# Loads of w_out earlier, two operands' low parts by DMA, another pool for a product's bank

## The chip, the cores and the metric

The kernel runs on one core of one Trainium2 chip. The metric is the device time of one execution in microseconds (us): 1637.95 us, the median of three runs (1635.71 to 1638.52).

## The reference, cut to what matters

One layer of a hybrid encoder block over 1024 tokens of width 1024, with 16 meta tokens ahead of them, all in float32. After the two mixers (an mLSTM, whose output is y_a, and neighbourhood attention, y_b) come the steps that the change touches:

```python
mix = g_a * (y_a @ w_branch_a) + g_b * (y_b @ w_branch_b)
h = h + mix @ w_out
z = rms_norm(h, norm2_g) @ w_ff1
h = h + jnp.square(jax.nn.relu(z)) @ w_ff2
```

In the kernel w_branch_a is `w_a`, w_branch_b is `w_b`, w_ff1 is `w1` and w_ff2 is `w2`.

## The kernel before, in words

**Products of three.** Every large product is made of matmuls of fp32r operands that are split into a high and a low part: high by high, high by low, low by high (`mm3`). The high part is a cast on ScalarE. The low part is made in one of two ways (`low`, L1157): VectorE subtracts the high part from the value, or ScalarE writes the negated high part and a DMA on POOL's queue adds the value to it in place (`by_dma`). `hilo` (L1151) makes both parts. For w_out's operands `Rows.split` (L1331) does the same; its DMA is L1338.

**Seven products for eight.** From w_a on, each product of matrices is done by a scheme of seven products (1 to 7) of half-sized operands. `ASIDE` names the left operand of each: A11, A12, A22 are quarters, S1 to S4 sums of quarters that `s_parts` (L1201) makes. `Cols` (L1227) handles one column block of w_a (four, `cols_a`) or w1 (sixteen, `cols_1`): a product is 12 matmuls into one bank of PSUM. `Rows` (L1314) handles w_out (`out_p`) and w2, each product in two halves q, of 24 matmuls into four banks.

**The order.** A list `seq` holds all these products as (object, i, q): 28 of w_a, then from n_o = 28 on 14 of w_out (1, 2, 6, 5, 3, 7, 4, each for q = 0 and 1), then from n_1 = 42 on those of w1, of whose first five blocks the products 1 and 2 come first. The loop at the end walks the list; before product n it runs what is hooked to n (`hook`, L1612), then has the operands of a few products ahead prepared (`ensure`, L1388), and then writes out the matmuls (`mul`). The operands of w_out are prepared from n_o on (`ready`), and in the kernel before this is also where w_out's eight loads are written (`Rows.load`, called by `parts`; `out_quarters`, L1463, with the load itself in L1470). x's first four loads (`load_x2`, L1476) are hooked to n_o - 7 to n_o - 4.

**The planner.** This order gives priorities only. A planner simulates the engines and queues when the program is built: it issues what is ready, by priority, and fixes the order on each engine and queue. The chip then works each queue strictly in that order. So a load can begin long before the place where it is written, once its buffer is free.

**Buffers.** Nearly all operands, loads and results live in 44 buffers of one kind (`slot`, 128 x 1040 values). PSUM has eight banks: a pool of two (`gbank`) and one of six (`bank`, also for the transposes and for w_out's four). `Cols.mul` takes its bank from the pool of two for the products 1 and 2.

**Ahead of w_a.** The eight blocks of w_b are multiplied by y_b in a loop over j. Their results go from PSUM into `gbq` on VectorE (`ev_b`, L1186), and after each second j to DRAM (`gbd<-gbq`, L1191). In the same loop y_a is loaded (`yq`, L1402), its quarters A11 (j = 3) and A12 (j = 4) are split (tiles `ya30`, `ya31`, `ya40`, `ya41`, with h or l), and from j = 5 on `s_parts` makes the sums (`ys`).

In the trace most instructions have the line of a helper, L137, and are told apart by tiles: `pow01l` is w_out's operand for q = 0, product 1, low part; `poz01l` the left one; `wo` are the raw loads.

Of the kernel before, what the change touches and what calls it, by code (L numbers as in the profile page):

```python
# [182 lines left out]
def build(tc, A, taps=None):  # L183
# [18 lines left out]
    def slot(name, dt=F32):  # L202
        return sp.tile([128, L], dt, name=name, tag="S")

    def bank(name="x"):
        return psx.tile([128, 512], F32, name=name, tag="x")

    def gbank(name="g"):
        return psg.tile([128, 512], F32, name=name, tag="g")
# [31 lines left out]
    def mm3(out, ah, al, bh, bl, first, last):  # L241
        PE.matmul(out, ah, bh, start=first, stop=False)
        PE.matmul(out, ah, bl, start=False, stop=False)
        PE.matmul(out, al, bh, start=False, stop=last)
# [154 lines left out]
    def gemm_block(wh, wl, n0, n, ks=KC, act=(xh, xl), off=0):  # L399
        ps = gbank()[:, 0:n]  # L400
        m = slice(n0 - off, n0 - off + n)
        for k in range(ks):
            c = slice(k * 128, (k + 1) * 128)
            mm3(ps, wh[:, c], wl[:, c], act[0][k][:, m], act[1][k][:, m], k == 0, k == ks - 1)
            yield 3 * n * 0.000422
        return ps

    def first_block(wh, wl, n0, n):

        ps = gbank()[:, 0:n]  # L410
        m = slice(n0, n0 + n)
        for k in range(KC):
            c = slice(k * 128, (k + 1) * 128)
            PE.matmul(ps, wh[:, c], xh[k][:, m], start=k == 0, stop=False)
            PE.matmul(ps, wh[:, c], xl[k][:, m], start=False, stop=False)
        for k in range(KC):
            ins = PE.matmul(ps, wl[:, k * 128:(k + 1) * 128], xh[k][:, m], start=False, stop=k == KC - 1)
        return ps, ins

    def gemm_in(wi, blocks, evac, ks=KC, act=(xh, xl), off=0, ahead=1):  # L420
        wh, wl = W.get(wi, ahead)
        for b, (n0, n) in enumerate(blocks):
            ps = yield from gemm_block(wh, wl, n0, n, ks, act, off)
            evac(b, n0, n, ps)

    def run(gen):
        while True:
            try:
                next(gen)
            except StopIteration as e:  # L430
                return e.value
# [23 lines left out]
    for b, ts in enumerate(groups):  # L455
        n0, n = b * 256, min(256, L - b * 256) if b < 3 else L - 768
        ps = run(gemm_block(gh, gl, n0, n))
# [5 lines left out]
        for j in (0, 1):  # L463
            ps, ins = first_block(*wx[j], n0, n)
# [89 lines left out]
    ya = {}  # L554
# [579 lines left out]
    def late(name, dt=F32):  # L1134
        return LP.tile([128, 1024], dt, name=name, tag="r", bufs=7)
# [6 lines left out]
    def lo(e):  # L1142
        return slice(e * 512, e * 512 + 512)
# [7 lines left out]
    def hilo(src, name, by_dma=False):  # L1151
        h_, l_ = slot(name + "h", F32R), slot(name + "l", F32R)
        SC.copy(h_[:, 0:S], src[:, 0:S])
        low(l_[:, 0:S], src[:, 0:S], h_[:, 0:S], by_dma)
        return h_, l_

    def low(l_, src, h_, by_dma):  # L1157
        if by_dma:

            SC.activation(l_, h_.bitcast(F32), AF.Copy, scale=-1.0)  # L1160
            nc.gpsimd.dma_start(l_, src, accum_op=OP.add)
        else:
            rest(l_, src, h_, share_gp[0])
# [9 lines left out]
    def load_gb(p):  # L1173
        for h_ in range(2):
            gb[p, h_] = slot(f"gbq{p}{h_}")
            dma(gb[p, h_][:, 0:1024].rearrange("p (e t) -> p e t", e=2),
                gated[2 * p:2 * p + 2, :, h_ * 512:h_ * 512 + 512].rearrange("e p t -> p e t"))
# [8 lines left out]
    def ev_b(j):  # L1186
        def ev(b, n0, n, ps):
            o = gb[j // 2, b][:, lo(j % 2)]
            V.scalar_tensor_tensor(o, o, 1.0, ps, OP.add, OP.mult)
            if j % 2 == 1:  # L1190
                dma(gbd[j // 2, b], gb.pop((j // 2, b))[:, 0:1024])  # L1191
        return ev
# [34 lines left out]
    class Cols:  # L1227
# [56 lines left out]
            return self.t["sp"]  # L1284

        def mul(self, i, q):
            ps = gbank("pf") if i in (1,2) else bank("pf")
            c = self.c.pop(i)
            for k in range(4):
                h_, l_ = self.z[ASIDE[i], k // 2]  # L1290
                m = lo(k % 2)
                mm3(ps, c[:, k * 128:(k + 1) * 128], c[:, 512 + k * 128:512 + (k + 1) * 128], h_[:, m], l_[:, m],
                    k == 0, k == 3)
            t = self.t
            if i == 1:
                pu = late("pu")
                t["p1"], t["u2"] = pu[:, 0:512], pu[:, 512:1024]
                SC.copy(t["p1"], ps)
            elif i == 2:
                self.out(0, 0, ps, t["p1"])  # L1300
            elif i == 6:
                V.tensor_add(t["u2"], ps, t["p1"])
            elif i == 7:
                t["u3"] = self.spare()[:, 0:512]
                V.tensor_add(t["u3"], ps, t["u2"])
            elif i == 5:
                self.out(1, 1, ps, t["u3"])
                V.tensor_add(t["u2"], ps, t["u2"])
            elif i == 4:
                self.out(1, 0, ps, t["u3"])  # L1310
            else:
                self.out(0, 1, ps, t["u2"])
# [72 lines left out]
    seq, before, after, ready = [], {}, {}, {}  # L1385
# [10 lines left out]
    za = {}  # L1396
    yq = {}

    def load_ya(h_):
        for i in range(4):  # L1400
            yq[h_, i] = slot(f"yq{h_}{i}")
            dma(yq[h_, i][:, 0:1024].rearrange("p (e t) -> p e t", e=2),  # L1402
                yad[2 * i:2 * i + 2, :, h_ * 512:h_ * 512 + 512].rearrange("e p t -> p e t"))
# [14 lines left out]
    for j in range(8):  # L1418
        if j == 7:
            cols_a[0].prep(2, 0)  # L1420
        if j in (1, 3):
            load_gb(j // 2 + 2)
        run(gemm_in(w_b[j], NBS, ev_b(j), 4, ([t[0] for t in ybs], [t[1] for t in ybs])))
        if j in (1, 2):
            load_ya(j - 1)
        if j in (3, 4):
            for i in (0, 1):
                za["A11" if j == 3 else "A12", i] = hilo(yq[0, 2 * (j - 3) + i], f"ya{j}{i}")
        if j >= 5:
            next(sy)  # L1430
    ybs = None
# [42 lines left out]
    def load_x2(t):  # L1474
        x_ = slot(f"hx{t}")
        dma(x_[:, 0:D], A["x"][t * 128:(t + 1) * 128, :])  # L1476
        hx.append(x_)
# [38 lines left out]
    out_p = Rows("po", out_quarters, out_o, late, True)  # L1516
# [95 lines left out]
    def hook(d, n, fn):  # L1612
        d.setdefault(n, []).append(fn)

    group(cols_a, NE1)
    n_o = len(seq)
# [20 lines left out]
    for t in range(4):  # L1637
        hook(before, n_o - 7 + t, lambda t=t: load_x2(t))
        hook(before, n_o + 2 + t, lambda t=t: load_x2(t + 4))
    ready[n_1] = n_o + 11  # L1640

    def z_half(k0):
        zt(0, range(k0, k0 + 4))
        for i in range(2):
            zz["A11" if k0 == 0 else "A12", i] = hilo(zf[0, k0 // 2 + i], f"za{k0}{i}")
# [98 lines left out]
```

## Time and profile before

| | us |
|---|---|
| median of three runs | 1637.95 |
| lowest and highest | 1635.71, 1638.52 |
| the profiled execution | 1635.56 |
| its span, first to last instruction | 1633.8 |
| TensorE busy in the span | 1589.9 (97%) |
| VectorE, ScalarE, POOL busy | 1129.7, 897.5, 231.1 |
| TensorE's granted clock, mean | 0.994 |

Times in the views are counted from the span's start. A busy TensorE is not TensorE at its peak. A wait is the idle time of an engine right before an instruction, put down to what ended last before it.

### The profile page before, as it was taken

To read this page: it belongs to the slowest core of one execution; us is meant where nothing else is said; L and a number is where in the kernel's file an instruction comes from. 1 tells how busy PE (TensorE), PEld (TensorE's weight loads), DVE (VectorE), ACT (ScalarE), POOL (GpSimd) and SP (SyncE) were. 2 spreads that over 40 slices of the span, in tenths; PEclk is the share of its full clock that TensorE was granted. 3 is DMA by queue.
4 is the path that set the end of the run, shared out by engine and by line. 5 is a ranking of instruction groups with operands and counts; after the bars stand their busy time and mean duration, and the time that the engine had idled before them with its cause. 6 is when DMAs were issued, how large, how long until landed. Compare 5 with 4: busy or idle time off the path is not lost.

```text
span 1633.8 us, 22503 instructions
## 1 busy us (share of the span) xinstructions
PE 1589.9 (97%) x8081; PEld 1351.2 (83%) x8081; DVE 1129.7 (69%) x2191; ACT 897.5 (55%) x1572; POOL 231.1 (14%) x387
## 2 busy tenths in 40 slices
PE   7999999999999999999999999999999999999999
PEld 7878889888989998888778788788888878888887
DVE  4537766574758687774398968965655595969597
ACT  5566676576748586864242656644444467344350
POOL 5110212112143223121100121000000001010000
PEclk9999999999999999999999999999999999999999
DMA  4362664636374444354933972133323639282733
GB/s 156 88 136 66 153 146 127 147 78 169 64 183 95 102 89 109 70 119 140 291 136 130 270 187 83 53 133 123 123 111 116 229 107 311 57 247 67 219 83 98
DMA packets 78415, 221.07 MB, mean 135 GB/s; under 512 B 11336, under 2 KB 21960, under 8 KB 78304
## 3 DMA queue, kind: packets, MB, share of 16 engines
q1 hardware_dynamic: 54976, 138.76, 24.3%
q0 software_dynamic: 23328, 80.88, 24.0%
q8 instruction: 64, 1.05, 0.3%
q14 instruction: 47, 0.39, 0.1%
HBM read 168.12 MB, written 38.76 MB: 127 GB/s over the span
## 4 chain that ended last, share of the span: by engine, by line
PE 79%; issue 8%; DMA 5%; ACT 4%; DVE 4%; POOL 1%; POOLq 0%; DVEq 0%; ACTq 0%
PE pf L137 41%; PE g L137 27%; DMA wl<-w_in 3%; PE po L137 2%; PE pt L137 2%; PE pp L137 1%; PE ps L137 1%; PE pi L137 1%; PE pn L137 1%; PE pu L137 1%; DMA xcl<-xc 1%; DVE gt L137 1%; DMA pow01l<-w_out 1%; PE pk L137 1%; PE pq L137 1%
## 5 line engine op out<-in xcount | busy, mean ns | idle before, releaser
L137 PE MATMUL g<-xh,wh 128*128 128x512 f32 (+3 forms) x784 | 290.7, 371 | 7.3 <-DVE xm L137 3.9
L137 PE MATMUL g<-xh,wl 128*128 128x512 f32 (+3 forms) x784 | 287.6, 367 | 5.4 <-DMA wl<-w_in 5.4
L137 PE MATMUL g<-xl,wh 128*128 128x512 f32 (+3 forms) x784 | 287.3, 366 | 0.0
L137 PEld LDWEIGHTS g<-xh,wh 128*128 128x128 f32 x784 | 148.9, 190 | 25.7 <-DVE xm L137 4.2
L137 PEld LDWEIGHTS g<-xh,wl 128*128 128x128 f32 x784 | 148.9, 190 | 25.0 <-DMA wl<-w_in 7.0
L137 PEld LDWEIGHTS g<-xl,wh 128*128 128x128 f32 x784 | 149.1, 190 | 16.8
L137 ACT ACTIVATE zq<-zq 128x512 f32<-128x512 f32 x128 | 80.7, 633 | 123.7 <-DVE zq L137 121.9
L137 DVE TENSOR_TENSOR acc<-acc,pf 128x512 f32<-128x512 f32 x96 | 64.1, 681 | 40.5 <-PE pf L137 40.3
L137 DVE CUSTOM_DVE_ANT_0 P<-ps,bt 128x400 f32<-128x400 f32 x64 | 36.0, 570 | 41.1 <-issue 24.2
L137 ACT ACTIVATE wl<-wh 128x1024 fp32r<-128x1024 f32 (+1 forms) x50 | 49.3, 987 | 24.1 <-DMA wh<-w_b 8.6
L174 POOL DMA_DIRECT2D wl<-w_in x42 | 38.4, 914 | 137.5 <-ACT wl L137 73.6
L137 DVE SCALAR_TENSOR_TENSOR C<-C,decb,pu 128x258 f32<-128x258 f32 x52 | 23.6, 479 | 39.3 <-PE pu L137 39.0
L137 DVE TENSOR_TENSOR pu<-pf,pu 128x512 f32<-128x512 f32 x40 | 27.4, 686 | 30.1 <-PE pf L137 30.0
L137 ACT ACTIVATE P<-P,mn 128x400 f32<-128x400 f32 x64 | 40.2, 630 | 10.9 <-DVE mn L137 10.4
L1338 POOL DMA_DIRECT2D f0w02l<-w_ff x1 | 0.9, 911 | 313.8 <-DVE zq L137 313.8
L137 DVE TENSOR_TENSOR zq<-pf,sp 128x512 f32<-128x512 f32 x32 | 22.1, 691 | 32.4 <-PE pf L137 32.4
L137 DVE TENSOR_SCALAR P<-P,sm 128x384 f32<-128x384 f32 (+1 forms) x128 | 38.5, 364 | 0.9
L137 DVE TENSOR_TENSOR zq<-pf,pu 128x512 f32<-128x512 f32 x32 | 22.0, 687 | 22.6 <-PE pf L137 22.6
L137 DVE TENSOR_TENSOR ptl<-pp,pth 128x384 fp32r<-128x384 f32 x64 | 35.5, 555 | 2.8 <-ACT pth L137 2.1
L137 ACT CAST pth<-pp 128x512 fp32r<-128x512 f32 x60 | 34.0, 581 | 5.4 <-PE pp L137 5.2
L137 PE MATMUL pp<-con,P 128*128 128x128 f32 x256 | 34.9, 272 | 0.0
L137 ACT ACTIVATE nn<-pi,tm 128x258 f32<-128x258 f32 x60 | 27.0, 473 | 14.1 <-PE pi L137 14.1
(2400 smaller groups left out, 4765.2 us busy)
## 6 DMA issues: line engine op xcount, KB each, us to landing
wh<-w_in POOLq DMA_DIRECT2D x42, 512.0 KB, 5.5
wl<-w_in POOLq DMA_DIRECT2D x42, 512.0 KB, 5.8
z2d<-zq SPq DMA_DIRECT2D x32, 512.0 KB, 3.0
zr<-z2d SPq DMA_DIRECT2D x32, 512.0 KB, 4.6
w2r<-w_ff SPq DMA_DIRECT2D x32, 512.0 KB, 13.0
bt<-rpbd SPq DMA_DIRECT2D x256, 32.0 KB, 2.8
xcl<-xc POOLq DMA_DIRECT2D x8, 520.0 KB, 5.2
ra<-rowd SPq DMA_DIRECT2D x8, 512.0 KB, 4.3
```

The costliest lines, as they stand in the source:

```text
L137: return fn(out, *a, **k)
L174: self.nc.gpsimd.dma_start(l[:, 0:w], src, accum_op=OP.add)
L1338: nc.gpsimd.dma_start(l_[:, 0:S], src, accum_op=OP.add)
```

## The change

It does three things. w_out's loads for q = 0 and q = 1 are hooked to the products n_o - 9 and n_o - 4. The low parts of A11 and A12 of y_a are made by ScalarE and a DMA on POOL's queue and not by VectorE: four times one negation and one transfer of 512 KB. And in `Cols.mul` product 2 takes its bank from the pool of six, so that the pool of two is left to product 1.

```diff
         def mul(self, i, q):
-            ps = gbank("pf") if i in (1,2) else bank("pf")
+            ps = gbank("pf") if i == 1 else bank("pf")
...
         if j in (3, 4):
             for i in (0, 1):
-                za["A11" if j == 3 else "A12", i] = hilo(yq[0, 2 * (j - 3) + i], f"ya{j}{i}")
+                za["A11" if j == 3 else "A12", i] = hilo(yq[0, 2 * (j - 3) + i], f"ya{j}{i}", True)
...
         hook(before, n_o - 7 + t, lambda t=t: load_x2(t))
         hook(before, n_o + 2 + t, lambda t=t: load_x2(t + 4))
     ready[n_1] = n_o + 11
+    for q in range(2):
+        hook(before, n_o - 9 + 5 * q, lambda q=q: out_p.load(q))
```

## Rows read from the trace of the kernel before

**Rows 1.** The page, part 1: span, and busy time of TensorE.

```profile
span 1633.8 us, 22503 instructions
...
PE 1589.9 (97%) x8081; PEld 1351.2 (83%) x8081; DVE 1129.7 (69%) x2191; ACT 897.5 (55%) x1572; POOL 231.1 (14%) x387
```

**Rows 2.** Waits of TensorE from 760 us to the end: us in total, times, longest us.

```profile
PE pf L137 <- ACT pow02h L137: 3.3, 1, 3.3
PE g L137 <- DVE gbq L137: 2.9, 4, 1.3
...
PE pf L137 <- ACT pu L137: 1.4, 2, 0.8
```

**Rows 3.** Timeline of TensorE, w_out's first products: start, us, instruction [idle before <-releaser].

```profile
911.78 1.09 PE L137 MATMUL pf<-pow01h,poz01h 128*128 128x512 f32 x4
916.13 0.49 PE L137 MATMUL pf<-pow02h,poz02h 128*128 128x512 f32 x1 [3.26 <-ACT pow02h L137]
916.90 0.50 PE L137 MATMUL pf<-pow01l,poz01h 128*128 128x512 f32 x1 [0.28 <-DMA pow01l<-w_out]
...
923.45 0.39 PE L137 MATMUL pf<-pow11l,poz11h 128*128 128x512 f32 x1
```

**Rows 4.** Stretches: length, busy PE, PEld, DVE, ACT, POOL; granted clock, DMA share, GB/s.

```profile
800.00:810.00 10.00, 8.80 (x38) 6.55 (x37) 5.20 (x6) 2.62 (x3) 0.87 (x1) 1.00 1.07 371
810.00:820.00 10.00, 8.65 (x38) 6.59 (x36) 7.48 (x9) 1.68 (x2) 1.41 (x2) 1.00 0.42 104
890.00:900.00 10.00, 10.00 (x45) 8.10 (x44) 7.77 (x13) 3.92 (x6) 0.00 (x0) 1.00 0.64 221
900.00:910.00 10.00, 10.00 (x45) 8.13 (x44) 9.66 (x12) 3.05 (x3) 0.86 (x1) 1.00 1.03 413
918.00:920.00 2.00, 2.00 (x6) 1.63 (x5) 2.00 (x4) 0.06 (x1) 0.43 (x1) 0.50 1.07 223
920.00:922.00 2.00, 2.00 (x7) 1.56 (x7) 1.97 (x3) 1.97 (x3) 0.00 (x0) 0.68 1.08 213
```

**Rows 5.** Timeline of SP's DMA issues, 893 to 912 us.

```profile
893.68 2.43 SPq L1476 DMA_DIRECT2D hx<-x  x3
...
897.17 2.28 SPq L1470 DMA_DIRECT2D wo<-w_out  x4
...
901.10 4.17 SPq L1470 DMA_DIRECT2D wo<-w_out  x4
```

**Rows 6.** Timeline of ScalarE, 897 to 916 us.

```profile
904.95 1.05 ACT L137 CAST pow01h<-wo 128x1024 fp32r<-128x1024 f32 x1 [5.81 <-DMA wo<-w_out]
```

**Rows 7.** Tile pow01l: its low-part transfer and its time to landing.

```profile
L1338 POOL DMA_DIRECT2D pow01l<-w_out x1: 861/861/861, 907.5 to 907.5; - x1
...
DMA to landing us min/median/max: 9.4/9.4/9.4
```

**Rows 8.** The same of tile pow11l.

```profile
L1338 POOL DMA_DIRECT2D pow11l<-w_out x1: 876/876/876, 914.6 to 914.6; - x1
...
DMA to landing us min/median/max: 7.2/7.2/7.2
```

**Rows 9.** Time to landing of tile pow06l's transfer.

```profile
DMA to landing us min/median/max: 4.5/4.5/4.5
```

**Rows 10.** Timeline of VectorE beside w_branch_b's products.

```profile
799.71 1.22 DVE L137 TENSOR_TENSOR ya31l<-yq,ya31h 128x1024 fp32r<-128x1024 f32 x1
800.85 0.68 DVE L137 SCALAR_TENSOR_TENSOR gbq<-gbq,g 128x512 f32<-128x512 f32 x1
...
812.58 1.23 DVE L137 TENSOR_TENSOR ys<-yq,yq 128x1024 f32<-128x1024 f32 x1 [2.52 <-DMA gbd<-gbq]
813.73 0.68 DVE L137 SCALAR_TENSOR_TENSOR gbq<-gbq,g 128x512 f32<-128x512 f32 x1
```

**Rows 11.** Timeline of TensorE there.

```profile
801.58 0.50 PE L137 MATMUL g<-yb0h,wh 128*128 128x512 f32 x1 [0.88 <-DVE gbq L137]
...
814.46 0.50 PE L137 MATMUL g<-yb0h,wh 128*128 128x512 f32 x1 [1.35 <-DVE gbq L137]
```

## The prediction

> **What bounds the kernel now.** I read the page first. TensorE is busy 1589.9 us of a span of 1633.8 [rows 1], so of the whole span only some 44 us can be won without taking work from it, and every other engine matters by the waits that it ends on TensorE. The second view is therefore TensorE's list of waits from 760 us on, where the changed code runs [rows 2]. The reader is to see three of them there: one of 3.3 us on pow02h, four on gbq (2.9 us together), two on pu (1.4 us). Each belongs to one part of the change.
>
> The third view is TensorE's timeline around w_out's first product [rows 3]. It begins at 911.78. Four products of high parts run, then the engine stands 3.26 us and 0.28 us more, because the low part pow01l comes only at 916.9. The wait has a tail that the list of waits does not show: in the stretch from 918 to 920 the granted clock is 0.50, which is 1.2 GHz in place of 2.4, and from 920 to 922 it is 0.68 [rows 4]. Before that the engine had stood for those 3.5 us; after the wait of 1.35 us at 814.46 [rows 11] the clock stayed at 1.00 [rows 4]. The tail costs 2 x 0.50 + 2 x 0.32 = 1.64 us. Wait and tail are 5.2 us.
>
> What ended that wait is read backwards. pow01l was issued at 907.5 and took 9.4 us [rows 7]; its high part was cast at 904.95, when the load had landed [rows 6]; the load was issued at 897.17, behind x's loads, which began at 893.68 [rows 5]. All these transfers ran into full DMA engines: 1.03 of them busy from 900 to 910, but only 0.64 from 890 to 900 [rows 4].
>
> **The change, part by part.** The sum is made against the profiled execution (1635.56 us for a span of 1633.8), which is 2.39 us below the median shown, 1637.95. A change of 0.2%, 3.3 us, is what a measurement of this kernel can tell from none.
>
> **A, w_out's loads.** No transfer is added; eight change their place in SP's order. The loads are hooked at products 19 and 24. They need buffers of the 44, and a buffer comes when a product gives it back, so the hook will not by itself move them nine products. I take it that the first four get the places from 893.68 on, which x's loads have now, 3.5 us earlier [rows 5]; x's loads move back by as much, and are used only after w_out's first product. SP's own issues cost nothing that anything waits for: about 0.4 us each, hidden by the transfers. A load took 904.95 - 897.17 = 7.8 us; with the same duration it lands at 901.5, cast, negation and issue take 907.5 - 904.95 = 2.55 us, and with the same 9.4 us the low part lands at 913.4. It is needed one matmul, 0.23 us, after 911.78 (10 us hold some 44 [rows 4]), at 912.0. That leaves 1.4 us of wait. At the 4.5 us that pow06l took when the loads were through [rows 9], it lands at 908.5 and leaves nothing.
>
> What is late next is pow11l, the second half's low part. It landed at 914.6 + 7.2 = 921.8 [rows 8]. If the first half runs without a wait, its 24 matmuls end at 917.3, and pow11l is needed at 917.5 and not at 923.45 [rows 3]: it must come 4.3 us sooner. Its load keeps its place as the second four (901.10, [rows 5]) behind the same number of transfers; what can bring it forward is the 3.6 us that the DMA engines left unused from 890 to 900. That leaves 0.7 us. The two waits don't add, since TensorE does not wait again for what it has lost already. I take 1.0 us, between 0.7 and 1.4, too short for the clock to fall. A is -5.2 + 1.0 = **-4.2**. The ends: -5.2, and 0.0 (pow11l no sooner at all: 923.45 - 921.8 = 1.6 won, the clock's 1.6 paid again).
>
> Here a rule bears on the sum. The low part took 4.5 to 9.4 us for 512 KB [rows 7 to 9]. The Trainium skill (DMA: Bandwidth & Descriptors, Anatomy of one DMA - SWDGE (gpsimd) path) gives such a transfer 2.0 us and its bytes at 436 GB/s, 3.2 us here. By that both low parts would be in time, and A would be -5.2. None of the three rows agrees.
>
> **B, the low parts of the first two operands.** Four subtractions of 1.22 us leave VectorE (ya31l at 799.71 is one, [rows 10]), 4.9 us. Beside the first two TensorE waited 0.88 us at 801.58 for an evacuation of gbq that stood behind ya31l [rows 10, 11]; I take 0.6 us of it as won, ends 0 and 0.9. The last two are off the path, as VectorE stood idle for 2.52 us behind them [rows 10]. Added are four negations on ScalarE, each at most 2.55 - 1.05 = 1.5 us, in a stretch where it is busy 2.62 of 10 us; four issues of 0.86 us on POOL [rows 7], ahead of w_branch_b's next loads, on an engine busy 0.87 of 10; and four transfers of 512 KB. If that cover failed, w_branch_b's low parts would be late by those issues, 3.4 us at most.
>
> The transfers are the cost that I can only bound. Plain loads ran at 413 GB/s with the DMA engines full (900 to 910), low parts at 223 and 213 with them as full (918 to 922) [rows 4], so one takes 1.3 to 2.4 us of all engines. Three of the four fall into a stretch that is full already, 1.07 from 800 to 810 [rows 4]. A store of gbq ends in that stretch, and ys on VectorE waits for the buffer that it gives back until 812.58, with an evacuation behind it at 813.73 [rows 10]; TensorE waits 1.35 us for that one [rows 11]. Each us that the store lands later is a us there. The ends are 0 and 3 x 2.4 = 7.2. I take three at the lower price, as the stretch is most like 900 to 910, and half of it for SP's transfers, as the two queues share the engines: 1.9 us. B is -0.6 + 1.9 = **+1.3**.
>
> **C, the second product's bank.** It adds no instruction. The two waits of 1.4 us together on pu [rows 2] are those of a second product of w_ff1 for a bank that a first product still holds. With six banks to choose from they go. The price is that the second product now shares those six with w_out's four and with the transposes, which the trace of before cannot show; its bound is another 1.4 us the other way. Nearest is the present state, in which TensorE waits for no bank of the larger pool there. C is **-1.4**, ends -1.4 and +1.4.
>
> The sum is -4.2 + 1.3 - 1.4 = -4.3: 1631.3 us for the profiled execution, **1633.7** for a median.
>
> **The rivals.** *The wait moves*: pow11l's load comes no sooner, TensorE stands at about 917.5 for as long as it now does at 913, and A is 0. For it: the same transfers go through the same full engines; against it: the 3.6 us unused. It gives 1.3 - 1.4 = -0.1, 1637.9.
>
> *The change doesn't do what it says*: the planner begins a load when its simulated buffer is free, and issued these at 897.17, five products before their place in the program. If SP's order stays as it is, A is 0 as well and the time 1637.9.
>
> *All is in time*: low parts need little of the engines, no wait is left, B costs nothing. -5.2 - 0.6 - 1.4 = -7.2, 1630.7.
>
> *Slower*: the added low parts hold back gbq's store with all four at 2.4 us, 9.6 us. VectorE stands at ys for that long, the evacuation behind it, and TensorE; a wait so long brings the clock's 1.6 us too. -4.2 - 0.6 - 1.4 + 9.6 + 1.6 = +5.0, 1643.0. It decides from a delay of 7.9 us on, where the sum passes +3.3. For it: full engines and an evacuation that stands behind ys. Against it: the share falls to 0.42 after 810, and the planner may put the evacuation ahead. The Trainium skill (DMA: Bandwidth & Descriptors, Issuing engines are not separate DMA queues) says that transfers of all queues run on the same 16 engines, which is this rival's ground; rows 4 agree.
>
> **How the numbers follow.** The forecast has 0.47 and *all in time* 0.08, together 0.55 for faster. *The wait moves* has 0.22 and *no new order* 0.09, together 0.31 for the same. *Slower* has 0.14. The range begins at 1630.7 less 1.5, as the three runs of before lie up to 2.2 us from their median: 1629.2. Upwards it takes in 1637.9 and about half the way on to 1643.0: 1640.5. The forecast's own range is 1630.7 to 1636.
>
> **What would show it.** A right: in SP's timeline four w_out loads stand ahead of x's, pow01l lands before 913.5, and the granted clock stays at 1.00 behind it. A wrong: a wait of over 3 us on pow11l. B right: no wait over 1 us at the w_branch_b product of 801, and ys begins before 815. B wrong: ys after 819. C right: no wait on pu near 1017. Any of it would be wrong as well if the planner, whose order changes as a whole from 793 us on, put new waits of over 2 us into w_a's products.

## The result, and the profile after

The kernel after takes 1651.66 us (median of four runs, 1648.03 to 1655.59), the one before beside it 1637.88 (four runs). The ratio is 1.0085, with a 95% interval from 1.0067 to 1.0102: 13.8 us slower, where 4.3 us faster were forecast. The profiled execution took 1648.03 us, the fastest of the four.

The page of the kernel after, its span and the engines' busy time:

```profile
span 1646.2 us, 22544 instructions
...
PE 1592.4 (97%) x8081; PEld 1354.3 (82%) x8081; DVE 1123.4 (68%) x2187; ACT 902.5 (55%) x1576; POOL 235.3 (14%) x391
```

Beside [rows 1], TensorE does the same 8081 matmuls. The span has grown by 12.4 us; VectorE has 6.3 us of work less (the four subtractions of 1.22 us among it), ScalarE 5.0 more and POOL 4.2. TensorE's waits from 760 us on, the answer to [rows 2]:

```profile
PE g L137 <- DVE gbq L137: 6.9, 4, 5.9
PE pf L137 <- ACT w10c L137: 5.8, 1, 5.8
PE pf L137 <- DMA pow12l<-w_out: 4.3, 1, 4.3
PE pf L137 <- DVE pu L137: 1.0, 1, 1.0
```

The waits on pow02h (3.3 us) and, in w_ff1, on pu (1.4 us) are gone, as the change meant. Three long ones stand in their place, one in the stage of each part.

**w_branch_b (part B).** The stores of gbq, from their issue to their landing: median 10.1 us before (shortest 4.7, longest 15.1), and after:

```profile
L1191 SPq DMA_DIRECT2D gbd<-gbq x4: 320/658/2419, 793.5 to 807.1; - x4
...
DMA to landing us min/median/max: 13.4/18.2/23.3
```

They are issued at the same time and land 8.1 us later. What stands behind them is seen in three timelines of the kernel after: ScalarE, VectorE, TensorE.

```profile
816.85 1.06 ACT L137 ACTIVATE ya41l<-ya41h 128x1024 fp32r<-128x1024 f32 x1 [8.65 <-DMA gbd<-gbq]
819.35 0.63 ACT L137 ACTIVATE wl<-wh 128x512 fp32r<-128x512 f32 x1 [1.44 <-DMA gbd<-gbq]
819.88 1.03 ACT L137 CAST ys10h<-ys 128x1024 fp32r<-128x1024 f32 x1
```

```profile
812.35 1.23 DVE L137 TENSOR_TENSOR ys<-yq,yq 128x1024 f32<-128x1024 f32 x1 [1.45 <-PE g L137]
...
820.94 1.23 DVE L137 TENSOR_TENSOR ys10l<-ys,ys10h 128x1024 fp32r<-128x1024 f32 x1 [5.63 <-ACT ys10h L137]
822.08 1.22 DVE L137 TENSOR_TENSOR yq<-ys,yq 128x1024 f32<-128x1024 f32 x1
823.22 0.68 DVE L137 SCALAR_TENSOR_TENSOR gbq<-gbq,g 128x512 f32<-128x512 f32 x1
```

```profile
823.96 0.79 PE L137 MATMUL g<-yb0h,wh 128*128 128x512 f32 x1 [5.92 <-DVE gbq L137]
```

The added negation of ya41 stands on ScalarE for 8.65 us, until a store gives back the buffer that it writes to; the cast of ys10h, whose operand was there at 813.6, stands behind it; ys10l on VectorE behind that; the evacuation of gbq behind ys10l; and TensorE waits 5.92 us. Its granted clock (third from the end in a row) falls to 0.50, which is 1.2 GHz. What that costs is the share of the clock that is missing, times the time that TensorE was busy (the second figure of a row), since a low clock costs nothing while the engine stands: 0.04 x 0.33 + 1.18 x 0.50 + 1.80 x 0.50 + 2.00 x 0.38 = 2.3 us more:

```profile
822.00:824.00 2.00, 0.04 (x1) 0.04 (x1) 2.00 (x4) 0.00 (x0) 0.00 (x0) 0.67 1.10 179
824.00:826.00 2.00, 1.18 (x2) 0.46 (x2) 2.00 (x2) 0.88 (x1) 0.00 (x0) 0.50 0.99 241
826.00:828.00 2.00, 1.80 (x4) 1.49 (x5) 2.00 (x4) 0.67 (x2) 0.00 (x0) 0.50 0.55 223
828.00:830.00 2.00, 2.00 (x7) 1.56 (x6) 1.04 (x1) 0.66 (x2) 0.86 (x1) 0.62 0.45 180
```

**w_out (part A).** SP's timeline shows the order that the change asked for, w_out's first four loads ahead of x's, in place of [rows 5]; and TensorE's shows the first product, the answer to [rows 3]:

```profile
898.67 1.96 SPq L1470 DMA_DIRECT2D wo<-w_out  x4
901.48 3.33 SPq L1476 DMA_DIRECT2D hx<-x  x4
904.91 1.38 SPq L1470 DMA_DIRECT2D wo<-w_out  x3
```

```profile
917.95 0.86 PE L137 MATMUL pf<-pow01h,poz01h 128*128 128x512 f32 x3
919.84 0.50 PE L137 MATMUL pf<-pow01h,poz01h 128*128 128x512 f32 x1 [1.03 <-DVE pu L137]
920.18 0.40 PE L137 MATMUL pf<-pow01l,poz01h 128*128 128x512 f32 x1
...
937.86 0.50 PE L137 MATMUL pf<-pow12l,poz12h 128*128 128x512 f32 x1 [4.34 <-DMA pow12l<-w_out]
```

The first wait is 1.03 us, and for a bank that VectorE empties late; low part pow01l is in time. But 18 us later TensorE stands 4.34 us for pow12l, and ScalarE's timeline tells why:

```profile
926.53 1.05 ACT L137 CAST poz12h<-ga 128x1024 fp32r<-128x1024 f32 x1 [8.05 <-DVE ga L137]
927.48 1.04 ACT L137 CAST pow12h<-wo 128x1024 fp32r<-128x1024 f32 x1
928.56 1.06 ACT L137 ACTIVATE pow12l<-pow12h 128x1024 fp32r<-128x1024 f32 x1
```

pow12h is w_out's own operand, but on ScalarE it stands behind poz12h, the left operand, which waits 8.05 us for one of w_a's last outputs (ga) from VectorE.

**w_ff1 (part C).** VectorE's timeline, first of the kernel before, then of the one after:

```profile
1007.18 0.69 DVE L137 TENSOR_TENSOR zq<-pf,pu 128x512 f32<-128x512 f32 x1
1010.12 1.23 DVE L137 TENSOR_TENSOR zs<-zf,zf 128x1024 f32<-128x1024 f32 x1 [2.25 <-ACT zf L137]
```

```profile
1023.51 0.69 DVE L137 TENSOR_TENSOR zq<-pf,pu 128x512 f32<-128x512 f32 x1 [7.96 <-issue]
1024.12 1.22 DVE L137 TENSOR_TENSOR zs<-zf,zf 128x1024 f32<-128x1024 f32 x1
```

zq sums up product 2 of the first block. TensorE computed that product from 1001.86 on before, 90.1 us behind w_out's first product, and now only from 1020.39 on, 102.4 us behind it:

```profile
1001.86 0.39 PE L137 MATMUL pf<-za40h,c 128*128 128x512 f32 x1
```

```profile
1020.39 0.48 PE L137 MATMUL pf<-za40h,c 128*128 128x512 f32 x1
...
1044.05 0.79 PE L137 MATMUL pf<-zs20h,w10c 128*128 128x512 f32 x1 [5.79 <-ACT w10c L137]
```

VectorE stands 7.96 us ahead of zq. The profile names no releaser there; that it is product 2 is read from the times, as zq starts at 1023.51, right behind that product's last matmul (1023.02). The sums for S1 and S2 stand behind zq in order, and at the end of the same row the sum `tt`, from which ScalarE casts w10c, an operand of w_ff1. For this cast TensorE stands 5.79 us, 20 us later.

### The profile page after: what moved, and what is told of

It reads as the page before. It is cut to its first block, busy times and chain, and to the rows that moved or that the text cites. A ratio compares the mean times of both kernels' runs of the same rounds, so it can differ in the third digit from the quotient of the medians.

```text
span 1646.2 us, 22544 instructions
## 1 busy us (share of the span) xinstructions
PE 1592.4 (97%) x8081; PEld 1354.3 (82%) x8081; DVE 1123.4 (68%) x2187; ACT 902.5 (55%) x1576; POOL 235.3 (14%) x391
## 3 DMA queue, kind: packets, MB, share of 16 engines
q8 instruction: 64, 1.05, 0.2%
## 4 chain that ended last, share of the span: by engine, by line
PE 74%; issue 11%; DMA 6%; DVE 4%; ACT 3%; POOL 1%; POOLq 0%; ACTq 0%; DVEq 0%
PE pf L137 40%; PE g L137 24%; DMA wl<-w_in 3%; PE po L137 2%; PE pt L137 1%; PE pp L137 1%; PE ps L137 1%; PE pi L137 1%; PE pn L137 1%; DMA xcl<-xc 1%; PE pu L137 1%; DMA ra<-masks 1%; DMA gbd<-gbq 1%; DVE gt L137 1%; DMA pow12l<-w_out 0%
## 5 line engine op out<-in xcount | busy, mean ns | idle before, releaser
L161 POOL DMA_DIRECT2D wh<-w_in x42 | 28.1, 669 | 44.2 <-PE pk L137 14.8
```

Source lines behind the costliest of these rows:

```text
L161: self.nc.gpsimd.dma_start(h[:, 0:src.shape[-1]], src)
```

## The experiments

The theory after this reading: each part damages its own stage, by a mechanism of its own, and A's own saving is real but passes to the next late operand. The table holds all runs; the experiments behind it refer to it. The stages are read from TensorE's timeline of each profile: *w_b* from the first matmul with yb0h to the first with wa0c, *w_a* from there to the first with pow01h, *w_out* from there to the first with w15c (w_out and the first five blocks of w_ff1). For the kernel before these starts are 782.82, 833.33, 911.78 and 1103.20. (The expectations count w_out's stage from its first to its last product alone: 88.3 us before, 90.5 after.)

| kernel | ratio to before, 95% interval | w_b | w_a | w_out |
|---|---|---|---|---|
| before | | 50.5 | 78.4 | 191.4 |
| after | 1.0085 (1.0067 to 1.0102) | 55.7 | 79.5 | 197.8 |
| after, again | 1.0087 (1.0070 to 1.0104) | 56.7 | 79.5 | 195.8 |
| A alone | 1.0003 (0.9990 to 1.0016) | 50.1 | 78.4 | 190.8 |
| B alone | 1.0039 (1.0027 to 1.0051) | 55.8 | 79.4 | 191.5 |
| C alone | 1.0023 (1.0007 to 1.0039) | 50.7 | 79.4 | 195.4 |
| A and B | 1.0039 (1.0025 to 1.0053) | 55.4 | 79.4 | 190.3 |
| A and C | 1.0024 (1.0009 to 1.0039) | 50.8 | 79.0 | 194.5 |
| B and C | 1.0074 (1.0052 to 1.0095) | 55.2 | 79.5 | 197.0 |
| B, 64 columns | 1.0000 (0.9988 to 1.0011) | 51.2 | 79.2 | 191.0 |
| B, A11 only | 1.0006 (0.9993 to 1.0018) | 51.6 | 79.2 | 191.5 |
| C, transposes later | 1.0022 (1.0006 to 1.0037) | 50.2 | 79.0 | 192.8 |
| C, not in five blocks | 0.9993 (0.9982 to 1.0004) | 51.0 | 79.2 | 191.5 |
| A, right first | 1.0005 (0.9991 to 1.0019) | 50.6 | 78.4 | 191.3 |
| A, right first, order of use | 0.9960 (0.9946 to 0.9973) | 50.1 | 78.5 | 186.8 |
| A, order of use | 0.9979 (0.9965 to 0.9992) | 50.5 | 78.5 | 187.9 |
| right first, order of use | 1.0003 (0.9992 to 1.0014) | 51.0 | 78.8 | 191.2 |
| order of use | 0.9994 (0.9981 to 1.0007) | 50.9 | 78.4 | 191.2 |

### Each part alone, and each taken out

A alone is before with the two lines of the hook:

```diff
+    for q in range(2):
+        hook(before, n_o - 9 + 5 * q, lambda q=q: out_p.load(q))
```

> Only w_out's loads are moved; y_a's low parts stay on VectorE and product 2 keeps the pool of two. Theory (each part does its own damage in its own stage): the wait on pow02h and pow01l (3.5 us and the clock's 1.6) goes, but a wait on the second product's low part pow12l comes, as in the kernel after (4.3 us and a fall of the clock), because VectorE's work on w_a's last outputs stands ahead of poz12h and poz12h stands ahead of pow12h on ScalarE. From w_out's first to its last product the kernel before took 88.3 us and the one after 90.5; the theory expects 89 to 91 here and a time 1 to 3 us over the kernel before. Rival (the earlier loads do save the 4.2 us that were forecast, and the wait on pow12l is a product of the other two parts, which shift VectorE's work): no wait over 1.5 us on pow12l, w_out's stage 84 to 86 us, the time 3 to 5 us under the kernel before.

B alone is before with

```diff
-                za["A11" if j == 3 else "A12", i] = hilo(yq[0, 2 * (j - 3) + i], f"ya{j}{i}")
+                za["A11" if j == 3 else "A12", i] = hilo(yq[0, 2 * (j - 3) + i], f"ya{j}{i}", True)
```

> Only the four low parts of A11 and A12 of y_a go by DMA. Theory: the four added transfers delay gbq's stores by some 8 us, ys10h on ScalarE stands behind a negation that waits for the store's buffer, VectorE's evacuation of gbq behind ys10l, and TensorE waits 5 to 6 us for it near 824, with the clock at 0.5 to 0.7 behind it; the time is 4.5 to 6 us over the kernel before, and w_out and w_ff1 take what they took before. Rival (the delay of the stores comes from the planner's other order of SP's loads, which all three parts change, and not from the added transfers): the stores land within 3 us of before, no wait over 2 us, the time within 1.5 us of the kernel before.

C alone is before with

```diff
-            ps = gbank("pf") if i in (1,2) else bank("pf")
+            ps = gbank("pf") if i == 1 else bank("pf")
```

> Only product 2's bank comes from the pool of six. Theory: the bank that product 2 of w_ff1's first block gets from the pool of six is one that the transposes of z hold before it, so that product 2 (za40) runs after four products of za0 and after the last transposes; VectorE's first sum (zq) waits 7 to 8 us for it with the sums for S1 and S2 queued behind it, and TensorE waits 5 to 6 us for w10c and S2 near 1032 to 1038, with the clock at 0.5 behind it; the two waits on pu are gone; the time is 3.5 to 5 us over the kernel before. Rival (the wait of 5.8 us comes from the lateness of w_out's last outputs, which part A made, and not from the bank): no wait over 2 us, the time 0 to 1.5 us under the kernel before.

The two other combinations leave out one of these diffs each (A and C has no B, A and B has no C).

> The change without its part B. Theory (the losses add, each in its own stage): 5 us less than the kernel after, that is 6 to 8 us over the kernel before; no wait over 2 us before 900, and both the waits on pow12l and on w10c stand. Rival (the wait on pow12l follows from the delay that part B makes): w_out's stage takes 84 to 86 us, only w10c's wait stands, and the time is within 1.5 us of the kernel before.

> The change without its part C. Alone, A measured 1.0003 and B 1.0039. Theory 1 (the parts act in separate stages and add): 1.004, that is 6 to 7.5 us over the kernel before; the wait on pow12l is 1.5 to 2.5 us as with A alone and the clock does not fall behind it. Theory 2 (A and B interact: the wait on pow12l is 4.3 us with a fall of the clock only where B has set VectorE's work on w_a's last outputs later): 4 us or more on pow12l, the clock at 0.5 to 0.7 behind it, 9 us or more over the kernel before.

B alone costs 0.39%, 6.4 us: w_b takes 5.3 us more, with the wait of 5.8 us on gbq. The time lies a little above the 4.5 to 6 us expected. C alone costs 0.23%, 3.8 us, and w_out takes 4.0 us more, with the wait of 5.8 us on w10c. Both losses fall in the stages where the theory put them. (w_a takes 0.5 to 1.1 us more in all versions with B or C; no experiment separates what does this.) TensorE's long wait with B alone, and with A alone the one on pow12l:

```profile
822.75 0.80 PE L137 MATMUL g<-yb0h,wh 128*128 128x512 f32 x1 [5.82 <-DVE gbq L137]
```

```profile
935.42 0.50 PE L137 MATMUL pf<-pow12l,poz12h 128*128 128x512 f32 x1 [1.87 <-DMA pow12l<-w_out]
```

A alone measured no change: the first wait is 1.05 us, the wait on pow12l 1.87, one of 0.37 on pow03l is new, the clock stays up, and the stage has won 0.6 us. The theory had asked for a loss of 1 to 3 us; the rival for a gain of 3 to 5. Neither came: A wins at the first product and gives it back behind it. A and C came to 3.9 us over before and not to the 6 to 8 expected: no wait on pow12l, whose transfer took 5.3 us there and not the 7.2 of A alone, and which TensorE reached later, after 1.7 us lost to the clock behind two short waits; nothing was won over C alone either. A and B came as the first theory had it, 2.47 us on pow12l without a fall of the clock.

> The change without its part A. Theory (what A wins at w_out's first product it gives back at pow12l): the sum of B and C alone, 1.0062, and not over 2.5 us from the kernel after in either direction; the wait on pow02h of 3 to 3.6 us and the clock's 1.7 are back, the wait on pow12l is gone. Rival 1 (A wins its 4 us also beside B and C): 1.009 or more. Rival 2 (A loses 2 us or more): 1.005 or less.

> The kernel after once more. The parts alone measured 1.0003, 1.0039 and 1.0023, together 1.0065; the kernel after measured 1.0085 with a wait of 4.3 us on pow12l and a fall of the clock behind it, while A and B together, with the same order of TensorE's matmuls there, had 2.5 us and no fall. Theory (the rest is chance: pow12l's transfer took 7.8 us in one profile and 6.3 us in the other, and a wait of that size only sometimes brings the clock down): the wait on pow12l is 1.5 to 4.5 us, and the ratio 1.006 to 1.008, with an interval that takes in the sum of the parts. Rival (all three parts together cost more than their sum): a wait of 4 us or more and the clock's fall again, the ratio 1.0085 or more.

Without A the change measured 1.0074, so A changes little beside the other parts either (the intervals overlap). The kernel after once more had 1.93 us on pow12l, not 4.34, as the theory had it: the transfer landed 18.0 us behind w_out's first product and not 19.9. The ratio, 1.0087, lies above the 1.006 to 1.008 that the theory expected, where the rival had it, and the clock fell again. Whether the parts add exactly stays open: alone they sum to 1.0065, and the root of the squares of their half widths (0.0013, 0.0012, 0.0016) is 0.0024, so that 1.0087 lies at the sum's upper end.

### What holds back the stores (part B)

```diff
-            nc.gpsimd.dma_start(l_, src, accum_op=OP.add)
+            nc.gpsimd.dma_start(l_[:, 0:64], src[:, 0:64], accum_op=OP.add)
```

(for the four transfers of B alone)

> B alone, but each of the four transfers adds only 64 of 1024 columns, so that the rest of these low parts is the negated high part; the negations, the issues and the waits for buffers are all there. Theory (the bytes of the added transfers hold back gbq's stores): the stores land within 2 us of before, the wait of 5.8 us for gbq's evacuation near 822 is under 1.5 us, and the time is 4.5 to 6 us under B alone, within 1.5 us of the kernel before. Rival (ScalarE's negations, standing in order ahead of other work until the store's buffer is free, are the cause, and the store is late for a reason other than bytes): the wait stays at 4 us or more and the time within 1.5 us of B alone.

And B for one operand of the two, `hilo(..., f"ya{j}{i}", j == 3)`:

> B for A11 alone (ya30 and ya31): two added transfers of 512 KB in place of four, both issued ahead of the last stores of gbq. Of the three that were ahead of the stores' landing with B alone, two are left. Theory (each 512 KB sets the stores back by its share of the engines, 8.1 us / 3 = 2.7 us each): the stores land 4.5 to 6.5 us later than before against w_b's products, TensorE waits 3 to 5 us for gbq's evacuation near 820 with the clock down behind it, and the time is 1.5 to 4.5 us over the kernel before. Rival (only the third transfer, ya40l, issued while the stores stand, holds them back): the stores land within 2 us of before, the wait stays under 2 us, and the time is within 1.5 us of the kernel before.

The same stores, from issue to landing, with 64 columns, and with two transfers in place of four (the line of B alone reads 13.6/18.2/23.8):

```profile
DMA to landing us min/median/max: 6.4/11.1/16.6
```

```profile
DMA to landing us min/median/max: 10.5/15.5/20.4
```

Against 10.1 us before, the median store is 1.0 us later with four transfers of 64 columns, 5.4 with two whole ones and 8.1 with the three that are ahead of it in B. That is 2.7 us for each 512 KB: the bytes hold back the stores, and the negations and issues, which are all there with 64 columns, account for 1.0 us at most. TensorE's longest wait on gbq was 3.1, 3.4 and 5.8 us. The wait with 64 columns missed its bound of 1.5. Against the 1.35 us before [rows 11] it grew by 1.75: TensorE got there 0.55 us sooner, since the wait of 0.88 us ahead of it had shrunk to 0.33, and the evacuation came 1.2 us later. The time with two transfers came out under the 1.5 to 4.5 us expected. In both versions the clock's 1.7 us stand behind the long wait, but the wait of 0.88 us is nearly gone and one of 1.6 us on wl is gone.

### What makes product 2 late (part C)

C alone, and

```diff
-    hook(before, n_1, lambda: zt(1, range(8)))
+    hook(before, n_1 + 2, lambda: zt(1, range(8)))
```

> C alone, and the transposes of z's second half are written two products later, behind the first two products of w_ff1, so that these take their banks of the pool of six ahead of the transposes. Theory (with C alone product 2 came late because its bank was one behind the transposes' in the pool's turn): product 2 (za40) runs before the second half's transposes again, VectorE does not stand 7 to 8 us before its first sum, the wait on w10c (5.8 us) and the clock's 3.4 us behind it fall under 1.5 us together, and the time is 3 to 5 us under C alone. Rival (product 2 is late because another instruction of the larger pool, not the transposes, holds the bank, or the sums are late of themselves): the wait on w10c stays over 4 us and the time is within 1.5 us of C alone.

Product 2 runs at 1006.94 again, ahead of the transposes, and VectorE goes through zq at 1012.60 without a wait. So it was the bank: product 2 had come behind the transposes in the larger pool's turn, and they wait for w_out's last outputs. But part of the loss stays, since the later transposes themselves now hold up the sums (VectorE waits 5.66 us for zf): 3.5 and 0.4 us on w10c in place of 5.8, and 1.5 us lost to the low clock while TensorE was busy, in place of 2.2 (both read in stretches of half a microsecond). The stage won 2.6 us of the 4.0, which is what these figures add up to. The 3 to 5 us that the theory expected did not come; the whole time (1.0022 against 1.0023) can't tell the two apart.

```profile
1012.60 0.69 DVE L137 TENSOR_TENSOR zq<-pf,pu 128x512 f32<-128x512 f32 x1
```

```profile
1038.88 0.50 PE L137 MATMUL pf<-zs20h,w10c 128*128 128x512 f32 x1 [3.47 <-ACT w10c L137]
```

```diff
+            ps = gbank("pf") if i == 1 or i == 2 and self.name in ("w10", "w11", "w12", "w13", "w14") else bank("pf")
```

> C alone, except that product 2 of w_ff1's first five blocks keeps the pool of two. Theory (all that C costs, and all that it wins, is in those five blocks): the two waits on pu (1.4 us) are back, the wait on w10c is gone, VectorE no longer stands 8 us before its first sum, and the time is within 1.5 us of the kernel before. Rival (C also costs in w_a's products or in the later blocks of w_ff1): 2 us or more over the kernel before, with a new wait outside the five blocks.

The two waits on pu are back, the wait on w10c is gone and the time is that of the kernel before: as far as it can tell, all of C, loss and gain, is in the five blocks.

### Where A's saving goes

```diff
+            w_first = self.name == "po" and i in (1, 2)
+            if not w_first:
                 self.z[q, i] = self.split(a, da, f"{self.name}z{q}{i}")
             self.w[q, i] = self.split(...)
+            if w_first:
+                self.z[q, i] = self.split(a, da, f"{self.name}z{q}{i}")
```

> A alone, and w_out's first two products have the right operand (pow) split before the left one (poz), so that on ScalarE the cast of pow12 no longer stands behind that of poz12, which comes 8.2 to 8.6 us after w_out's first product in every kernel so far, whatever the loads do, since it waits for w_a's last output from VectorE. Theory (A's saving went into a wait on pow12l that this order on ScalarE sets): pow12l is issued at least 5 us sooner against w_out's first product (12.1 us behind it with A alone) and no wait over 0.5 us on it is left; 2 to 4 us under A alone, 1.5 to 3.5 us under the kernel before. Rival (the full DMA engines set pow12l's landing): it lands within 2 us of A alone and the wait stays at 1.5 us or more; the time is within 1 us of A alone.

pow12l is issued 8.2 us sooner and lands 5.1 us sooner, and the wait on it is gone. The time did not move, against the theory's 2 to 4 us. TensorE's timeline, 48.6 us behind w_out's first product:

```profile
962.96 0.50 PE L137 MATMUL pf<-pow03l,poz03h 128*128 128x512 f32 x1 [2.54 <-DMA pow03l<-w_out]
```

The whole saving stands at pow03l now, with the clock's 1.7 us. pow03l landed 48.5 us behind the first product before, 49.2 with A alone, 48.5 here. Its issue comes at the end of ScalarE's row of ten operands (three instructions of about 1 us each), which starts when VectorE has made its sums of w_a's outputs (poz16h, the second of the ten, waits 5.46 us for them in this run). Before, TensorE needed it 2.1 us after it landed, so this was all that A could win, whatever it did at the first product. But ScalarE prepares 7 and 4 ahead of their use by 20 us and more, so the row can be put in the order of use:

```diff
+            if self.name == "po":
+                rest5 = [rest5[k] for k in (0, 2, 4, 1, 3)]
```

(`rest5` is the list of `parts`, for the products 6, 7, 5, 4, 3)

> A with the right operand first, and w_out's last five operands are prepared in the order in which TensorE uses them (6, 5, 3, 7, 4 in place of 6, 7, 5, 4, 3). With the right operand first the wait had moved on to pow03l (2.5 us and the clock's 1.7), which lands 48.5 to 49.2 us behind w_out's first product in every kernel so far, at the end of a ScalarE that prepares ten operands at 2.98 us each, though pow07, pow17, pow04 and pow14 come 20 to 33 us before they are used. Theory (A's saving was passed from one late operand to the next, and the row ends here): pow03l lands 8 us or more sooner, no wait over 1 us on a w_out operand is left, the clock stays at 1.00, w_out's stage (88.3 us before) takes 83 to 85, the time is 3.5 to 5.5 us under the kernel before. Rival (the stage is bound by VectorE's work on w_a's last outputs, and another wait of 2 to 3 us takes its place): the stage stays over 86.5 us, the time within 2 us of the kernel before.

> The kernel before with only the order in which w_out's last five operands are prepared changed to that of their use. Theory (in the kernel before pow03l has 2.1 us to spare and the wait is at the first product alone): nothing is won, the first wait of 3.3 us and its clock stay, w_out's stage within 0.7 us of 88.3, the time within 1.5 us of the kernel before. Rival (this order is worth something of itself): 2 us or more under the kernel before.

A, the right operand first and the order of use together take 0.40% less than before, 6.6 us (1631.6 against 1638.21), the lowest ratio measured; w_out's stage in the table is 4.6 us shorter. pow03l is issued at 944.2, 32.7 us behind the first product and not 41.6, and the clock stays at 1.00; w_out takes 83.0 us from its first to its last product, with the order of use alone 87.3. That order alone measured 0.9994, no change, with the first wait of 3.5 us and its clock still there. TensorE's timeline of this version, and what is left of its waits from 760 us on:

```profile
911.58 1.09 PE L137 MATMUL pf<-pow01h,poz01h 128*128 128x512 f32 x4
913.22 0.50 PE L137 MATMUL pf<-pow01l,poz01h 128*128 128x512 f32 x1 [0.54 <-DMA pow01l<-w_out]
```

```profile
PE g L137 <- DVE gbq L137: 2.9, 4, 1.4
PE pf L137 <- ACT pu L137: 1.4, 2, 0.8
...
PE pf L137 <- DMA pow01l<-w_out: 0.5, 1, 0.5
```

> The right operand first and the order of use, without A: w_out's loads stay where they were in the kernel before. Theory (A is the part that takes the first wait away, the other two only keep it from coming back): the wait of 3.3 us at the first product and the clock's 1.7 stay, w_out's stage is 87 to 89 us, the time within 2 us of the kernel before. Rival (the order on ScalarE was the cause, and A was not needed): w_out's stage under 85 us, the time 4 us or more under the kernel before.

> A and the order of use, with the left operand first as in the kernel before. Theory (the wait on pow12l comes from poz12h ahead of pow12h on ScalarE and only the right operand first takes it away): a wait of 1.5 to 2.5 us on pow12l stays, no wait on pow03l, w_out's stage 84.5 to 86.5 us, the time 1.5 to 4.5 us under the kernel before, between it and the version with all three. Rival (the order of use alone is enough): no wait over 1 us, the time 5 us or more under the kernel before.

Without A nothing is won (3.6 us on pow01l). This wait also bears out a reading of the prediction: [rows 3] put the first wait down to pow02h, and the prediction to the late pow01l; here, with no pow02h ahead of it, the same wait stands on pow01l itself. Without the right operand first, 0.21% are: no wait on pow12l in that profile, against the theory, since its transfer took 5.1 us there, and 7.8 and 6.3 in the two profiles with the longest waits on it. So A and the order of use carry the gain; what the right operand first adds (0.9960 against 0.9979) lies inside the overlap of the intervals.

## Why the prediction was wrong, by its steps

**A: the first wait right, the next one named wrong.** The first four loads took x's places, pow01l landed 2.1 us behind the first product and not 5.1 [rows 3, 7], and wait and tail of 5.2 us shrank to about 1.0. The step that failed is "What is late next is pow11l". pow11l was late in no version with A. The next late was pow12l, and behind it pow03l, whose lateness does not come from w_out's loads: ScalarE takes its work in order, and their place there is set by w_a's outputs. The Trainium skill (PSUM — Partial Sum Buffer, Engine vs sequencer instructions) calls ScalarE's queue strictly first in, first out; the run with the right operand first agrees, with a cast that could run 8.2 us sooner as soon as it did not stand behind poz12h. The prediction looked one operand ahead; the slack of each operand along the stage (pow12l 0.8 us, pow03l 2.1 us in the kernel before) would have shown that 4.2 us could not be won. In sum A was worth 0 (1.0003), where the forecast had -4.2 and its upper end 0.0.

**B: a price too small, and the rival's mechanism.** The gain was right: the wait of 0.88 us [rows 11] became 0.33. The step that failed is "I take three at the lower price ... and half of it for SP's transfers, as the two queues share the engines: 1.9 us". The stores were set back by 8.1 us, 2.7 for each transfer: a price above the upper one of 2.4 taken from [rows 4], and the stores bore it whole, where the forecast had half of the lower one. The Trainium skill (DMA: Bandwidth & Descriptors, Issuing engines are not separate DMA queues) has transfers of all engines run on the same 16 and interleave; the runs agree, as transfers on POOL's queue held back the stores on SP's. So it went as in the rival *slower*, to which 0.14 was given: a late store, an engine in order behind its buffer, an evacuation, TensorE, the clock. Only the engine was another: ys did start at 812.35, and it was ya41l's negation on ScalarE that stood. The prediction had costed these negations at nothing since ScalarE was idle, and had not asked what buffer they write to. Nor did "Each us that the store lands later is a us there" hold: TensorE's wait grew from 1.35 to 5.92 us, by 4.6 and not by 8.1, and the low clock cost 2.3 us, not 1.6. B came to +6.4 us, not +1.3.

**C: the wait went, the order broke.** No wait on pu is left in w_ff1, as forecast. The step that failed is its bound, "another 1.4 us the other way", taken from the size of the present waits. What changed was a turn: in the pool of six product 2 queues behind the transposes, so the order on TensorE changed, and with it VectorE's in-order row. With the transposes written later, 2.6 us of the stage's 4.0 came back; for the other 1.4 the profile shows the sums waiting for zf, which the transposes feed, but no run tests it. C came to +3.8 us, not -1.4. The prediction did say that new waits of over 2 us from the planner's other order would make it wrong, but looked for them in w_a's products, not here.

The sum, -4.3, had three terms, and all were too low: by 4.7 (A, against the 0.5 us of 1.0003), 5.1 (B) and 5.2 (C). That is 15.0 of the 18.1 us between the forecast and the result, which lies above the range (up to 1640.5) and above the slowest rival (1643.0). The other 3.1 us belong to no part alone, and whether they are more than noise stays open.

Most of the signs that the prediction named for its being right came true all the same: x's loads went behind w_out's first four, the clock stayed at 1.00 behind the first wait, no wait over 1 us stood at the product of 801, ys began before 815, and no wait on pu was left in w_ff1. They watched the waits that the change was to remove; the new ones stood behind other instructions.

## What to carry to other kernels

Before a wait is costed as won, list for the operands behind it when each lands and when it will be needed once that wait is gone: the smallest slack along the stage is the most that can be won, and what sets the landing there (here the order on ScalarE) is the thing to change with it. When a transfer is put into a stretch with full DMA engines, cost it in full (here 2.7 us for each 512 KB) at whoever waits for a transfer there, and follow it to TensorE through every in-order engine that stands behind that buffer. Taking a buffer from another pool changes whose turn it stands in; look for what holds that turn before counting free places.

## What the runs showed of the hardware

The clock's price of a short wait is not fixed. A and C together, and A with the order of use (left operand first), have the same two waits, 1.06 and 0.61 us, at w_out's first product. The granted clock behind them, first of A and C, then of the other (the third number from the end):

```profile
917.00:919.00 2.00, 2.00 (x7) 1.51 (x5) 2.00 (x4) 0.00 (x0) 0.00 (x0) 0.50 1.08 287
919.00:921.00 2.00, 2.00 (x8) 1.58 (x7) 1.93 (x4) 0.00 (x0) 0.00 (x0) 0.68 1.01 264
```

```profile
915.00:917.00 2.00, 2.00 (x10) 1.63 (x9) 2.00 (x3) 0.00 (x0) 0.00 (x0) 1.00 1.03 266
917.00:919.00 2.00, 2.00 (x11) 1.61 (x10) 1.93 (x4) 0.00 (x0) 0.00 (x0) 1.00 1.04 274
```

It fell to 1.2 GHz once and not the other time; nor did it fall behind 2.47 us with A and B, while it did behind 1.93 us in the kernel after's second profile. At one and the same product of w_branch_b it fell behind 1.79 us with C alone and not behind 1.96 us with A and C. The runs of one kernel spread by some 10 us (the kernel before 1631.82 to 1642.19 in 31 runs), and the start of w_branch_b, behind which all edits lie in the program, fell between 781.6 and 788.4 us. A stage's length in the profile told smaller differences apart than the whole time did.
